# Attention probabilities transposed in 32x32 squares on VectorE and placed by SBUF-to-SBUF DMAs

## The chip, the cores and the metric

One Trainium2 chip; the kernel runs on one of its cores. The metric is the device time of one execution in microseconds (us), as the median over runs. The engines are TensorE (PE, its weight loads PEld), VectorE (DVE), ScalarE (ACT), GpSimd (POOL) and SyncE (SP, which issues the DMAs here).

## The reference

A trunk of two encoder layers on 512 tokens of 1024 features, in float32. In each layer one projection feeds three attention branches with heads of 64 features: A (4 heads, all 512 keys with a mask made of three dilated windows), B (8 query heads over 2 key heads, all keys, normalized and rotated queries and keys) and C (4 heads on an 8 x 64 grid, a window of 16 columns, learned bias). The branches are projected to 1024 features, gated, added up and projected again; a layer norm follows, then an MLP of 4096 hidden features and a second layer norm.

```
s = q @ k.T (+ mask or bias);  p = exp(s - max(s));  p = p / sum(p);  o = p @ v
merged = g0 * (oa @ w_branch_a) + g1 * (ob @ w_branch_b) + g2 * (oc @ w_branch_c)
x = layer_norm(alpha * x + merged @ w_out);  x = layer_norm(alpha * x + relu(x @ w_up)**2 @ w_down)
```

## The kernel before

Each float32 operand is split into a high part of TensorE's type F32R and the remainder (`Split`, hi and lo), and a product is three matmuls (`mm3`, lines 152 to 155). Weights come in chunks of 512 KB (`Stream`): SyncE loads a chunk into one of two raw buffers, ScalarE copies the high part (line 182), VectorE subtracts it (line 183). `advance`, called whenever a chunk is taken, splits one more chunk if a buffer is free; a chunk that is asked for and not ready is split on the spot. There are 5 split chunks in the pool `wts` and 3 in a second pool that exists outside attention only.

Attention in a layer goes through 64 slots in the order of a list: heads of A, then C, then B, and in each head four blocks of 128 queries. The order of instructions on every engine is that of the program. A slot does this, in order: the scores of the slot two ahead (`scores`: two matmuls, maximum on VectorE, exponential and sum on ScalarE); one chore; other matmul work (`work.pump(rate)`: projections, gates and branch products of A and C, in units of one `mm3`); the normalization of the tile two ahead (on GpSimd in A and B, on VectorE in C); in the first slot of a head the products with the values of the head before (`values`, 8 matmuls); the transposition of this slot's tile (`turn`); then again a chore and work. The rate is the number of units per call: 2.1 in A, 2.85 in C, 1.6 in B.

`turn` transposes each 128x128 block of the probabilities on TensorE into a PSUM bank (line 544; 4 blocks in A and B, 2 or 3 in C); ScalarE copies it out as `pth`, VectorE subtracts into `ptl`. Both tiles hold a whole head and have one buffer. `values` multiplies them with the values, and ScalarE and VectorE add up the two halves of the result into `of`. What is left of the work list runs after the last slot; then `tail` computes B's gates and products for each block of 128 features, with the last head's `values` after its fourth matmul step. GpSimd adds the gated branches up (line 617, `mg`). Then come the output projection and the MLP (`token_major` and the loop from line 838).

```
normalize = ahead(i + 2); chores.pump(); work.pump(rate[name]); normalize()
if qb == 0 and i: values(*slots[i - 1][:2])
turn(name, h, qb, probs.popleft())
chores.pump(); work.pump(rate[name])
```

Of the kernel before, what the change touches and what calls it, by code (L numbers as in the profile page):

```python
# [28 lines left out]
RAWS = 2  # L29
NEG = -1e30  # L30
# [98 lines left out]
def encoder(ctx: ExitStack, tc: tile.TileContext, x, x_t, w_qkv, w_c, w_gate, b_gate, qn, kn, rpb,  # L129
# [34 lines left out]
    class Stream:  # L164
# [10 lines left out]
        def split(self):  # L175
            raw, more, _ = self.issued.popleft()
            pool, n = (extra[0], 3) if more else (wts, 5)
            self.used[more] += 1
            hi = pool.tile([P, 1024], F32R, tag="whi", name="whi", bufs=n)
            lo = pool.tile([P, 1024], F32R, tag="wlo", name="wlo", bufs=n)  # L180
# [17 lines left out]
        def advance(self):  # L198
# [3 lines left out]
            while n and self.issued and self.issued[0][2] < self.turn:  # L202
                more = self.issued[0][1]
                if self.used[more] == (5, 3)[more]:
                    break
# [89 lines left out]
    def attention(l, keep, qk, open_heads):  # L295
# [16 lines left out]
        def project(n, evac, cost, before=None, order=None):  # L312
# [4 lines left out]
            for tb, i in order:  # L317
# [6 lines left out]
                for j in range(per):  # L324
                    k = i * per + j
                    mm3(ps[tb], xT[:, tb, k], w[i][:, j], k == 0, k == KB - 1)
                    yield cost
                if i == nw - 1:
                    if tb == TB - 1:
                        for c in w:  # L330
                            stream.free(c)
# [86 lines left out]
        def c_values(m):  # L418

            while m == 0 and "a" not in flags:  # L420
# [86 lines left out]
        def scores(name, h, qb):  # L507
# [9 lines left out]
            if name == "b":  # L517
                s = ps
                nc.vector.tensor_reduce(st[:, 0:1], ps, axis=AX.X, op=ALU.max)
            else:  # L520
                s = p
                add = maska[:, (3 - qb) * P:(3 - qb) * P + S] if name == "a" else bias[h][:, C_OFF[qb]:C_OFF[qb] + n]
                nc.vector.tensor_tensor_reduce(s, ps, add, 1.0, -3e38, ALU.add, ALU.max, st[:, 0:1])
            nc.vector.tensor_scalar(st[:, 1:2], st[:, 0:1], -1.0, None, op0=ALU.mult)
            nc.scalar.activation(p, s, AF.Exp, bias=st[:, 1:2], accum_out=st[:, 2:3])
# [23 lines left out]
        def values(name, h):  # L549
            v = {"a": lambda: V["a"][h // 2][:, :, h % 2], "b": lambda: V["b"][:, :, h // 4],  # L550
                 "c": lambda: V["c", h // 2][:, :, h % 2]}[name]()
            pt = pts["now"]
            po = bank("pso")
            order = (1, 2, 0, 3) if name == "c" else range(TB)
            for i, kb in enumerate(order):
                q0, q1 = keys_of(name, kb)
                sl = slice(q0 * P, q1 * P)
                nc.tensor.matmul(po[:, sl], v[:, kb], pt.hi[:, kb, sl], start=i == 0, stop=False, skip_group_check=True)
                nc.tensor.matmul(po[:, sl], v[:, kb], pt.lo[:, kb, sl], start=False, stop=i == TB - 1, skip_group_check=True)
# [4 lines left out]
            dst, a, b = of[half:half + HD], po[:HD], po[HD:]  # L564
            if name == "c":
                dst = by_columns(dst)
                a, b = blocks(a), blocks(b)
            nc.scalar.activation(dst, a, AF.Copy)
            nc.vector.tensor_tensor(dst, dst, b, op=ALU.add)
# [43 lines left out]
        def gated(name, m):  # L613
            t = keep.tile([P, S], F32, tag="t", name="t", bufs=2)
            yield from gate({"b": 1, "c": 2}[name], m, t)
            yield from branch(name, m, t)
            nc.gpsimd.tensor_tensor(merged[m], merged[m], t, op=ALU.add)

        def branch_c():
            for m in range(KB):  # L620
# [50 lines left out]
        rate = {"a": 2.1, "c": 2.85, "b": 1.6}  # L671
# [28 lines left out]
        for i, (name, h, qb) in enumerate(slots):  # L700
# [20 lines left out]
        stream.plan([a for m in range(KB) for a in g(1, [m]) + ([w_bb[l, m // 2]] if m % 2 == 0 else [])])  # L721

        def tail():
            steps = 0
            for m in range(KB):
                for _ in gated("b", m):
                    steps += 1
                    if steps == 4:
                        values(*slots[-1][:2])
# [36 lines left out]
    stream.plan([w_qkv[0, i] for i in range(6)])  # L766
# [15 lines left out]
    for l in range(L):  # L782
        with ExitStack() as left:
# [13 lines left out]
            stream.plan([w_out[l, k] for k in range(KB)], [0] * 4 + [1] * 3 + [0])  # L797
            for half in range(2):
                more = [int(m % 8 in (1, 4, 6)) for m in range(16)]
                stream.plan([w_up[l, half * 16 + m] for m in range(16)], more)  # L800
                stream.plan([w_down[l, half * 16 + m] for m in range(16)], more[:12] + [1] * 3 + [0])
            if l < L - 1:
                stream.plan([w_qkv[l + 1, i] for i in range(6)])
# [190 lines left out]
```

## Time and profile before

| | |
|---|---|
| Median of 3 runs | 1546.78 us (1545.64 to 1905.47) |
| Profiled execution | 1549.4 us, span 1547.6 us |
| TensorE busy | 1527.6 us, 7400 matmuls, mean granted clock 0.996 |
| VectorE, ScalarE, GpSimd busy | 866.0, 632.5, 182.0 us |
| DMA | 150.61 MB, mean 97 GB/s |

The span goes from the first to the last instruction, and the profiled execution's own time is 1.8 us more. Busy times of different engines overlap and do not add up; a busy TensorE may still hold pipelined matmuls with gaps too small to show. An idle engine costs nothing unless the one that ends the work waits for it. In layer 0 the slots of A run from about 53 to 121 us, those of C to 199, those of B to some 310; layer 1 repeats this from about 818.

### The profile page before, as it was taken

To read this page: it belongs to the slowest core of one execution; us is meant where nothing else is said; L and a number is where in the kernel's file an instruction comes from. 1 tells how busy PE (TensorE), PEld (TensorE's weight loads), DVE (VectorE), ACT (ScalarE), POOL (GpSimd) and SP (SyncE) were. 2 spreads that over 40 slices of the span, in tenths; PEclk is the share of its full clock that TensorE was granted. 3 is DMA by queue.
4 is the path that set the end of the run, shared out by engine and by line. 5 is a ranking of instruction groups with operands and counts; after the bars stand their busy time and mean duration, and the time that the engine had idled before them with its cause. 6 is when DMAs were issued, how large, how long until landed. Compare 5 with 4: busy or idle time off the path is not lost.

```text
span 1547.6 us, 19148 instructions
## 1 busy us (share of the span) xinstructions
PE 1527.6 (99%) x7400; PEld 1279.8 (83%) x7400; DVE 866.0 (56%) x1498; ACT 632.5 (41%) x1036; POOL 182.0 (12%) x190
## 2 busy tenths in 40 slices
PE   8999999999999999999999999999999999999997
PEld 6888888888898888888888888888888888888886
DVE  4678877644664314441566787776448542244315
ACT  4665666533144212431136556665332431134310
POOL 0113213211100000000102141233111000000001
PEclk9999999999999999999999999999999999999999
DMA  6222311153153323332331323112432432233311
GB/s 218 83 85 75 111 55 58 52 177 123 55 177 96 96 82 96 110 96 83 106 128 56 98 82 103 55 59 95 146 123 83 136 99 92 82 123 95 96 55 55
DMA packets 43434, 150.61 MB, mean 97 GB/s; under 512 B 5072, under 2 KB 5712, under 8 KB 43344
## 3 DMA queue, kind: packets, MB, share of 16 engines
q1 hardware_dynamic: 43344, 149.40, 30.5%
q8 instruction: 58, 0.95, 0.2%
q14 instruction: 32, 0.26, 0.1%
HBM read 145.19 MB, written 4.19 MB: 97 GB/s over the span
## 4 chain that ended last, share of the span: by engine, by line
PE 95%; DVE 2%; ACT 1%; DMA 1%; issue 0%; POOL 0%; SPq 0%; POOLq 0%; DVEq 0%; ACTq 0%
PE psd L155 9%; PE psd L154 9%; PE psd L153 9%; PE psu L154 8%; PE psu L155 8%; PE psu L153 8%; PE psg L155 6%; PE psg L154 6%; PE psg L153 6%; PE psp L544 3%; PE psq L155 2%; PE psq L153 2%; PE psq L154 2%; PE psb L155 2%; PE psb L153 2%; PE psb L154 2%
## 5 line engine op out<-in xcount | busy, mean ns | idle before, releaser
L183 DVE TENSOR_TENSOR wlo<-raw,whi 128x1024 fp32r<-128x1024 f32 (+1 forms) x246 | 306.9, 1248 | 421.5 <-ACT whi L182 420.5
L182 ACT ACTIVATE whi<-raw 128x1024 fp32r<-128x1024 f32 (+1 forms) x246 | 258.4, 1053 | 462.8 <-PE psd L155 143.1
L153 PE MATMUL psu<-xTh,whi 128*128 128x512 f32 (+1 forms) x576 | 210.8, 366 | 0.0
L154 PE MATMUL psu<-xTl,whi 128*128 128x512 f32 (+1 forms) x576 | 210.7, 366 | 0.0
L155 PE MATMUL psu<-xTh,wlo 128*128 128x512 f32 (+1 forms) x576 | 210.5, 365 | 0.0
L153 PE MATMUL psd<-whi,hh 128*128 128x512 f32 x512 | 199.3, 389 | 0.0
L155 PE MATMUL psd<-whi,hl 128*128 128x512 f32 x512 | 199.2, 389 | 0.0
L154 PE MATMUL psd<-wlo,hh 128*128 128x512 f32 x512 | 199.2, 389 | 0.0
L153 PE MATMUL psg<-xTh,whi 128*128 128x512 f32 x384 | 156.8, 408 | 0.0
L154 PE MATMUL psg<-xTl,whi 128*128 128x512 f32 x384 | 151.6, 395 | 0.0
L155 PE MATMUL psg<-xTh,wlo 128*128 128x512 f32 x384 | 151.6, 395 | 0.0
L154 PEld LDWEIGHTS psu<-xTl,whi 128*128 128x128 f32 x576 | 108.6, 189 | 17.7
L153 PEld LDWEIGHTS psu<-xTh,whi 128*128 128x128 f32 x576 | 108.6, 189 | 17.4
L155 PEld LDWEIGHTS psu<-xTh,wlo 128*128 128x128 f32 x576 | 108.6, 189 | 17.4
L266 POOL TENSOR_TENSOR ve<-ve,nhalf 128x1 f32<-128x1 f32 x16 | 24.2, 1513 | 775.0 <-DVE ve L265 775.0
L529 POOL TENSOR_SCALAR p<-p,stat 128x512 f32<-128x512 f32 x96 | 70.7, 737 | 360.2 <-DVE stat L528 242.9
L154 PEld LDWEIGHTS psd<-wlo,hh 128*128 128x128 f32 x512 | 96.1, 188 | 20.0
L153 PEld LDWEIGHTS psd<-whi,hh 128*128 128x128 f32 x512 | 96.1, 188 | 19.9
L155 PEld LDWEIGHTS psd<-whi,hl 128*128 128x128 f32 x512 | 96.1, 188 | 19.8
L153 PE MATMUL psq<-whi,xTh 128*128 128x512 f32 (+1 forms) x256 | 90.0, 351 | 7.2 <-ACT whi L182 6.7
L229 DVE TENSOR_TENSOR ptl<-psp,pth 128x512 fp32r<-128x512 f32 (+2 forms) x128 | 81.6, 637 | 21.2 <-ACT pth L228 19.8
L155 PE MATMUL psq<-whi,xTl 128*128 128x512 f32 (+1 forms) x256 | 87.9, 343 | 0.0
(116 smaller groups left out, 2572.7 us busy)
## 6 DMA issues: line engine op xcount, KB each, us to landing
raw<-in_w_up SPq DMA_DIRECT2D x64, 512.0 KB, 3.6
raw<-in_w_down SPq DMA_DIRECT2D x64, 512.0 KB, 3.5
raw<-in_w_gate SPq DMA_DIRECT2D x48, 512.0 KB, 3.5
raw<-in_w_qkv SPq DMA_DIRECT2D x22, 512.0 KB, 3.6
raw<-in_w_out SPq DMA_DIRECT2D x16, 512.0 KB, 3.6
raw<-in_w_c SPq DMA_DIRECT2D x12, 512.0 KB, 3.5
bias<-in_rpb SPq DMA_DIRECT2D x8, 640.0 KB, 3.9
raw<-in_w_bb SPq DMA_DIRECT2D x8, 512.0 KB, 3.6
```

The costliest lines, as they stand in the source:

```text
L153: nc.tensor.matmul(ps, lhs.hi, rhs.hi, start=start, stop=False)
L154: nc.tensor.matmul(ps, lhs.hi, rhs.lo, start=False, stop=False)
L155: nc.tensor.matmul(ps, lhs.lo, rhs.hi, start=False, stop=stop)
L182: nc.scalar.activation(hi[:, s], raw[:, s], AF.Copy)
L183: nc.vector.tensor_tensor(lo[:, s], raw[:, s], f32(hi[:, s]), op=ALU.subtract)
L229: nc.vector.tensor_tensor(dst.lo, ps, f32(dst.hi), op=ALU.subtract)
L266: nc.gpsimd.tensor_tensor(ve[:, 1:], ve[:, :1], nhalf[:, :1], op=ALU.pow)
L529: (nc.vector if name == "c" else nc.gpsimd).tensor_scalar(p, p, st[:, 3:4], 1.0, op0=ALU.mult, op1=ALU.mult)
L544: nc.tensor.transpose(ps[:, j * P:(j + 1) * P], p[:, j * P:(j + 1) * P], ident)
```

## The change

`turn` issues one VectorE transpose in squares of 32x32 from the probabilities into a tile `tx` (two of them, heads taking turns). After a head's fourth slot `gather` issues 16 DMAs of 64 KB (32 partitions, 4 pieces of 512 B each) on SyncE, which put the squares into their places in `ptl` (one buffer). In the second and third slot of the next head `settle` makes the high part from it: ScalarE copies into the `tx` tile just read, GpSimd subtracts in place. In the fourth slot `values` follows, just before the next `gather`; the last head's has two of B's gates ahead of it in `tail`, with DMAs on SyncE and ScalarE and half the subtractions on VectorE. For C GpSimd clears the squares outside the keys. The maximum is taken with its sign changed, which drops one VectorE instruction a slot, and C is normalized on GpSimd too. The weights have 4 + 4 split buffers in place of 5 + 3, and a chunk of a projection is freed as soon as its last use is issued. The rates are 2.75 in C and 1.5 in B.

```diff
-            pool, n = (extra[0], 3) if more else (wts, 5)
+            pool = extra[0] if more else wts
...
-                nc.vector.tensor_reduce(st[:, 0:1], ps, axis=AX.X, op=ALU.max)
+                nc.vector.tensor_reduce(st[:, 1:2], ps, axis=AX.X, op=ALU.max, negate=True)
...
-                (nc.vector if name == "c" else nc.gpsimd).tensor_scalar(p, p, st[:, 3:4], 1.0, op0=ALU.mult, op1=ALU.mult)
+                nc.gpsimd.tensor_scalar(p, p, st[:, 3:4], 1.0, op0=ALU.mult, op1=ALU.mult)
...
             if qb == 0:
-                pts["now"] = Split(pool.tile([P, TB, S], F32R, tag="pth", name="pth", bufs=1),
-                                   pool.tile([P, TB, S], F32R, tag="ptl", name="ptl", bufs=1))
-            pt = pts["now"]
+                pts["at"] = pts.get("at", 0) ^ 1
+                pts["sq"] = pool.tile([P, TB * 4, TB, SQ], F32, tag=f"tx{pts['at']}", name="tx", bufs=1)
...
+                            nc.gpsimd.memset(pts["sq"][:, 4 * kb:4 * kb + 4, a:b], 0.0)
             k0, k1 = keys_of(name, qb)
-            n = k1 - k0
-            ps = bank("psp")[:, :n * P]
-            for j in range(n):
-                nc.tensor.transpose(ps[:, j * P:(j + 1) * P], p[:, j * P:(j + 1) * P], ident)
-            split_psum(pt[:, k0:k1, qb * P:(qb + 1) * P], ps.rearrange("p (k q) -> p k q", q=P))
+            nc.vector.transpose(pts["sq"][:, 4 * k0:4 * k1, qb], p.rearrange("p (c a) -> p c a", a=SQ))
+
+        def gather(name, h, queues):
+            lo = pool.tile([P, TB, S], F32R, tag="ptl", name="ptl", bufs=1)
+            pts["lo"], pts["of"] = lo, pts["at"]
+            for n in range(16):
+                i, j = n % 4, n // 4
+                dst = f32(lo)[j * SQ:(j + 1) * SQ].rearrange("a k (i r) -> a k i r", i=4)[:, :, i]
+                src = pts["sq"][i * SQ:(i + 1) * SQ].rearrange("a (k j) q b -> a k j (q b)", j=4)[:, :, j]
+                queues[n % len(queues)].dma_start(dst, src)
...
+        def settle(name, kbs, engines=(nc.gpsimd, nc.gpsimd)):
+            if kbs[0] == 0:
+                pts["hi"] = pool.tile([P, TB, S], F32R, tag=f"tx{pts['of']}", name="pth", bufs=1)
+            for kb in kbs:
+                q = keys_of(name, kb)
+                hi, lo = (by_squares(pts[n][:, kb], *q) for n in ("hi", "lo"))
+                nc.scalar.activation(hi, f32(lo), AF.Copy)
+                engines[kb % 2].tensor_tensor(lo, f32(lo), f32(hi), op=ALU.subtract)
...
-            if qb == 0 and i:
-                values(*slots[i - 1][:2])
-                if (name, h) == ("a", 2):
-                    flags.add("a")
             turn(name, h, qb, probs.popleft())
+            if i >= TB:
+                before = slots[i - TB][:2]
+                if qb in (1, 2):
+                    settle(before[0], ((0, 1), (2, 3))[qb - 1])
+                if qb == TB - 1:
+                    values(*before)
+                    if before == ("a", 1):
+                        flags.add("a")
+            if qb == TB - 1:
+                gather(name, h, (nc.sync,) if i < len(slots) - 1 else (nc.sync, nc.scalar))
```

## Rows read from the trace of the kernel before

**Rows 1.** The page, part 1: busy time of each engine, share of the span.

```profile
PE 1527.6 (99%) x7400; PEld 1279.8 (83%) x7400; DVE 866.0 (56%) x1498; ACT 632.5 (41%) x1036; POOL 182.0 (12%) x190
```

**Rows 2.** The page, part 4: the chain of waits by line.

```profile
PE psd L155 9%; PE psd L154 9%; PE psd L153 9%; PE psu L154 8%; PE psu L155 8%; PE psu L153 8%; PE psg L155 6%; PE psg L154 6%; PE psg L153 6%; PE psp L544 3%; PE psq L155 2%; PE psq L153 2%; PE psq L154 2%; PE psb L155 2%; PE psb L153 2%; PE psb L154 2%
```

**Rows 3.** Busy time by stage, layer 0: heads A, C, B (window, us, engines, clock).

```profile
53.00:121.00 68.00, 67.92 (x374) 58.46 (x375) 48.87 (x120) 41.86 (x84) 10.44 (x16) 0.97 0.25 80
121.00:199.00 78.00, 78.00 (x388) 65.31 (x387) 63.36 (x151) 46.28 (x92) 22.81 (x22) 1.00 0.29 88
199.00:299.00 100.00, 100.00 (x501) 82.59 (x500) 74.50 (x152) 61.10 (x120) 28.45 (x34) 1.00 0.18 57
```

**Rows 4.** TensorE in order of time in B: start, us, engine, line, operation.

```profile
205.50 0.40 PE L155 MATMUL psb<-oh,wlo 128*128 128x512 f32 x1
205.73 0.60 PE L544 MATMUL psp<-ident,p 128*128 128x128 f32 x4
206.09 0.48 PE L153 MATMUL psb<-oh,whi 128*128 128x512 f32 x1
206.40 0.39 PE L154 MATMUL psb<-ol,whi 128*128 128x512 f32 x1
```

**Rows 5.** Waits of TensorE: who for whom, total us, times, longest.

```profile
PE psp L544 <- POOL p L529: 4.6, 2, 2.3
```

**Rows 6.** Busy time by 1 us after the first turn, with granted clock (PEclk).

```profile
54.00:55.00 1.00, 1.00 (x4) 0.81 (x3) 0.59 (x1) 0.37 (x1) 0.36 (x1) 0.50 0.91 348
...
56.00:57.00 1.00, 1.00 (x4) 0.81 (x3) 0.19 (x3) 0.74 (x2) 0.00 (x0) 0.50 0.00 0
```

**Rows 7.** Groups by line and shape: xcount, busy us, mean ns, idle before.

```profile
L183 DVE TENSOR_TENSOR wlo<-raw,whi 128x1024 fp32r<-128x1024 f32 x242 | 304.2, 1257 | 420.3 <-ACT whi L182 419.3
L182 ACT ACTIVATE whi<-raw 128x1024 fp32r<-128x1024 f32 x242 | 255.8, 1060 | 461.4 <-PE psd L155 143.1 <-DMA raw<-in_w_up 88.7 <-PE psu L154 87.6
...
L529 POOL TENSOR_SCALAR p<-p,stat 128x512 f32<-128x512 f32 x96 | 70.7, 737 | 360.2 <-DVE stat L528 242.9 <-DVE stat L524 90.9 <-PE pss L514 8.2
L229 DVE TENSOR_TENSOR ptl<-psp,pth 128x512 fp32r<-128x512 f32 x96 | 66.1, 689 | 20.4 <-ACT pth L228 19.5
...
L519 DVE TENSOR_REDUCE stat<-pss 128x1 f32<-128x512 f32 x64 | 43.8, 685 | 3.7 <-PE pss L514 3.3
...
L617 POOL TENSOR_TENSOR mg<-mg,t 128x512 f32<-128x512 f32 x32 | 43.8, 1369 | 158.6 <-DVE t L607 158.6
L228 ACT ACTIVATE hh<-r 128x512 fp32r<-128x512 f32 x64 | 40.4, 631 | 77.4 <-DVE r L844 77.4
```

**Rows 8.** Line 617 on GpSimd: duration ns minimum, median, maximum.

```profile
L617 POOL TENSOR_TENSOR mg<-mg,t x32: 1270/1290/2204, 234.7 to 1143.8; 128x512 f32<-128x512 f32 x32
```

**Rows 9.** GpSimd and VectorE in order of time after B's last head.

```profile
310.68 1.22 DVE L183 TENSOR_TENSOR wlo<-raw,whi 128x1024 fp32r<-128x1024 f32 x1
...
310.85 2.20 POOL L617 TENSOR_TENSOR mg<-mg,t 128x512 f32<-128x512 f32 x1 [4.23 <-DVE t L607]
```

**Rows 10.** SyncE's issues in order of time: start, us, tile, count.

```profile
783.53 0.40 SPq L655 DMA_DIRECT2D gqk<-in_qn  x1
...
784.97 0.38 SPq L501 DMA_DIRECT2D bias<-in_rpb  x1
```

**Rows 11.** DMA issues by tile: count, KB each, median us to landing.

```profile
x_dram<-x SPq DMA_DIRECT2D x8, 256.0 KB, 2.0
...
gqk<-in_qn SPq DMA_DIRECT2D x2, 64.0 KB, 3.9
```

**Rows 12.** First matmuls of `values`: a head's in A, C, B, B's last but one.

```profile
68.55 0.40 PE L558 MATMUL pso<-pth,v 128*128 128x512 f32 x1
...
120.91 0.40 PE L558 MATMUL pso<-pth,v 128*128 128x512 f32 x1
...
198.56 0.34 PE L558 MATMUL pso<-pth,v 128*128 128x384 f32 x1
...
299.27 0.39 PE L558 MATMUL pso<-pth,v 128*128 128x512 f32 x1
```

More of the change, by code (lines that the diff above doesn't have):

```diff
@@ L29 @@
 RAWS = 2
+AHEAD = 4
+FIRST = [1, 1, 0, 0, 0, 0]
+SQ = 32
 NEG = -1e30
@@ L203, in advance @@
                 more = self.issued[0][1]
-                if self.used[more] == (5, 3)[more]:
+                if self.used[more] == AHEAD:
                     break
@@ L418, in c_values @@
         def c_values(m):
-            while m == 0 and "a" not in flags:
+            while m == 0 and "a" not in flags or m == 1 and ("a", 1) not in oT:
                 yield None
@@ L556, in values @@
                 q0, q1 = keys_of(name, kb)
-                sl = slice(q0 * P, q1 * P)
-                nc.tensor.matmul(po[:, sl], v[:, kb], pt.hi[:, kb, sl], start=i == 0, stop=False, skip_group_check=True)
-                nc.tensor.matmul(po[:, sl], v[:, kb], pt.lo[:, kb, sl], start=False, stop=i == TB - 1, skip_group_check=True)
+                to = by_squares(po, q0, q1)
+                for n in ("hi", "lo"):
+                    nc.tensor.matmul(to, v[:, kb], by_squares(pts[n][:, kb], q0, q1), start=(i, n) == (0, "hi"),
+                                     stop=(i, n) == (TB - 1, "lo"), skip_group_check=True)
             half = (h % 2) * HD
@@ L565, in values @@
             if name == "c":
[L566 to L569, printed above, removed]
+                to = dst.rearrange("p (i r q c) -> p i r q c", i=4, r=2, q=TB)
+                cut = [(lambda t, r=r: t.rearrange("p (i q r c) -> p i r q c", i=4, q=TB, r=2)[:, :, r], to[:, :, r])
+                       for r in range(2)]
+            else:
+                cut = [(lambda t: by_squares(t, 0, TB), dst.rearrange("p (q i b) -> p i q b", q=TB, i=4))]
+            for f, to in cut:
+                nc.scalar.activation(to, f(a), AF.Copy)
+                nc.vector.tensor_tensor(to, to, f(b), op=ALU.add)
             if half:
@@ L619, in branch_c @@
         def branch_c():
+            while ("c", 1) not in oT:
+                yield None
             for m in range(KB):
@@ L720, in attention, with drain @@
         work.flush()
-        stream.plan([a for m in range(KB) for a in g(1, [m]) + ([w_bb[l, m // 2]] if m % 2 == 0 else [])])
-        def tail():
-            steps = 0
+        stream.plan(g(1, (0, 1)) + [w_bb[l, 0]])
+        stream.plan([a for m in range(2, KB) for a in g(1, [m]) + ([w_bb[l, m // 2]] if m % 2 else [])])
+        def drain(gen):
+            while True:
+                try:
+                    next(gen)
+                except StopIteration as e:
+                    return e.value
+        def tail():
+            last = slots[-1][:2]
+            settle(last[0], (0, 1), (nc.vector, nc.gpsimd))
+            ts = [drain(half_gate("b", 0))]
+            settle(last[0], (2, 3), (nc.vector, nc.gpsimd))
+            ts.append(drain(half_gate("b", 1)))
+            values(*last)
             for m in range(KB):
[L726 to L729, printed above, removed]
+                drain(gated("b", m, ts[m]))
+                if m + 2 < KB:
+                    ts.append(drain(half_gate("b", m + 2)))
                 yield merged[m]
@@ L765, in encoder @@
     xp = right.enter_context(tc.tile_pool(name="x", bufs=1, side="right", reuse_waits="tile"))
-    stream.plan([w_qkv[0, i] for i in range(6)])
+    extra[0] = right.enter_context(tc.tile_pool(name="early", bufs=1, side="right", reuse_waits="tile"))
+    stream.plan([w_qkv[0, i] for i in range(6)], FIRST)
     def split_x(tb, t, cut):
@@ L796, in encoder @@
             extra[0] = pool(right, "wts", "right")
-            stream.plan([w_out[l, k] for k in range(KB)], [0] * 4 + [1] * 3 + [0])
+            stream.plan([w_out[l, k] for k in range(KB)], [0, 1] * 4)
             for half in range(2):
-                more = [int(m % 8 in (1, 4, 6)) for m in range(16)]
-                stream.plan([w_up[l, half * 16 + m] for m in range(16)], more)
-                stream.plan([w_down[l, half * 16 + m] for m in range(16)], more[:12] + [1] * 3 + [0])
+                stream.plan([w_up[l, half * 16 + m] for m in range(16)], [0, 1] * 8)
+                stream.plan([w_down[l, half * 16 + m] for m in range(16)], [0, 1] * 8)
             if l < L - 1:
-                stream.plan([w_qkv[l + 1, i] for i in range(6)])
+                stream.plan([w_qkv[l + 1, i] for i in range(6)], FIRST)
             with ExitStack() as inner:
```

31 lines of the change are left out of this document (20 added, 11 removed).

## The prediction

> **What bounds the kernel now.** I read the busy times first: TensorE is busy for 99% of the span, and no other engine passes 56% [rows 1]. Busy can hide pipelining, so the chain of waits came next. Its sixteen costliest entries are all TensorE's, and the transposes of the probabilities (line 544) stand among them with 3% [rows 2]. The table by stage says the same of heads A, C and B: TensorE fills each stretch, and the fullest other engine is VectorE in C with 63.4 of 78 us [rows 3]. Whatever leaves TensorE comes off the end, until a new wait appears.
>
> **What is removed.** In the order of time, a group of four transposes takes 0.36 us before the next matmul starts, and that matmul runs 0.08 us longer than its neighbours' pitch of 0.23: 0.44 us a group, 0.11 a transpose [rows 4]. A layer has 64 in A, 40 in C (2 or 3 key blocks) and 128 in B: 232, with both layers 464, so 464 x 0.11 = **-51 us**; the chain's 3% of the span, 46, bears it out. The matmuls of `values` keep their number and columns.
>
> At the first turn of each layer TensorE waits for GpSimd's normalized tile, 4.6 us over both [rows 5], and then runs at the lower of its two levels, a granted clock of 0.50 (1.2 GHz) for some 3 us, losing about 1.5 us [rows 6]. Behind the transposes stood gate work that needs no probabilities, so this goes: 4.6 + 3 = **-7 us** (bounds 0 and -8).
>
> **What moves to other engines, at nothing while its cover holds.** VectorE loses the subtractions into `ptl` (0.69 us each) and gets one transpose per slot. The trace has no such transpose; the nearest rows are the one-input reduction of the same tile (0.69) and the 1024-column subtraction (1.26); I take 0.69, so its load hardly moves. ScalarE keeps four copies a head, at 0.63 from SBUF. GpSimd gets four subtractions a head at the `mg` addition's price, 1.29 us at the median and 1.37 on average, beside four normalizations at 0.74, and C's too [rows 7, 8]. TensorE's work in the slots is the cover for all of this; without it GpSimd's 5.2 us a head would be bare, which is what happens below.
>
> **Weights.** One split chunk fewer is ready during attention. `project` for the queries of B holds all four while it runs; the chunk after it is split only when it is asked for, which puts a copy of 1.06 and a subtraction of 1.26 [rows 7] in front of TensorE: up to 2.3 us in each layer, **+4 us** (bounds 0 and 5). Elsewhere two chunks stay ready, 16 units of three matmuls at 0.70 us, or 11 us. The 4 + 4 split in the MLP keeps as many chunks, and I cost it at nothing: the gaps it could open lie behind 4 ready chunks.
>
> **The new loop.** This decides. A head's 16 transfers write `ptl`, which has one buffer, so they wait until `values` of the head before has read it. `values` of this head then waits for the transfers, for ScalarE's copies and for GpSimd's subtractions. Nothing in that ring overlaps with itself, so successive heads cannot come closer than its length. SyncE waits there too: weight loads issued later stand behind its 16 transfers, up to 7.5 us, which the ready chunks cover. Its parts:
>
> - Transfers. Four issues that follow each other on SyncE start at 783.53 to 784.97, 0.48 us apart on average [rows 10]; I take 0.47. The last lands 2.0 us after its issue, as `x_dram<-x` does (SBUF as source, nothing ahead of it); `gqk`, 64 KB like these, needed 3.9 behind other loads [rows 11]. 15 x 0.47 + 2.0 = 9.05 us. Bounds: 7.7 (an issue's own 0.38, 2.0) and 11.0 (0.47, 3.9).
> - Settling. First copy 0.63 and a hand-over taken as 0.1, four subtractions at 1.29 in a row, one normalization of 0.74 that stands between the pairs in GpSimd's order: 6.6. Later gate additions and VectorE in the way: 0.4 more (bounds 0 and 1.4). 7.0.
> - The last matmul and its end, and SyncE's start: 0.23 + 0.39 = 0.6.
>
> Together **16.65 us** (C's last head has 10 of 16 blocks, so 2.0 less). Against it stands the time TensorE needs for a head. The first matmuls of `values` lie 17.45 us apart in A (three heads), 19.41 in C (four), 14.39 in B (seven) [rows 12]. Less the transposes (1.76, 1.10, 1.76) and, in C and B, four times 0.2 unit at 0.70 that the lower rate defers: 15.69, 17.75 and **12.07**. The deferred work runs later at the same cost. So C hides the loop, A nearly does, and B does not. In a layer, eight gaps between successive `values` fall into B's slots, one of them behind C's last head, and two into A's: 7 x (16.65 - 12.07) + (14.65 - 12.07) + 2 x (16.65 - 15.69) = 36.6 us, with both layers **+73 us**. A lower clock after such waits would cost about 1.5 us a head, inside the wait, so I add nothing.
>
> **Sum.** Against the profiled execution's 1549.4: -51 - 7 + 4 + 73 = 1568.4. That execution lies 2.6 us above the runs' median of 1546.78, so I predict **1566 us**, 1.2% slower: the gain is spent on waits in the B heads. With the lower bound of the transfers the loop is 15.3 and costs 46, or 1539.
>
> **Rivals.**
>
> *The loop is hidden.* If the transfers were issued much closer together or landed sooner, so that the ring fits into 12.1 us, only -51 - 7 + 4 remains: 1493 us, 3.5% faster. For it: TensorE now needs nothing from GpSimd to proceed within a head, and the slots have work. Against it: 5.2 us of subtractions and 0.6 of copy leave under 6 us for 16 issues that take 7 by [rows 10]. It needs overlap that I did not see; a part of it lies between 1493 and 1516 with a loop below 14.
>
> *The loop is longer, and the kernel slower.* Transfers of 128 pieces of 512 B land like `gqk`, 3.9 us after issue: the loop is 18.55. Then B loses 45.4 + 4.5, A 5.7 and C 4 x 0.8 = 3.2 a layer, 118 in all: 1610 us. The verdict turns at a loop of 17.2 us, where the sum passes 1578; that is 0.6 above my value. For it: GpSimd's additional work meets VectorE, and weight loads share the DMA engines. Against it: `gqk` queued behind larger loads.
>
> *GpSimd is blocked by VectorE.* The `mg` addition that started 0.17 us into a weight subtraction took 2.20 us, where 1.29 is usual [rows 9]: 0.9 lost. With about one and a half weight subtractions in a head's time, at worst 1.4 us join the loop, of which I have counted 0.4: +1.0 x 10 gaps x 2 = 20 us more, 1586. The Trainium skill (SBUF — State Buffer, Who interferes with whom) gives a rule by which a VectorE instruction with two SBUF inputs and a GpSimd instruction that reads SBUF exclude each other for a whole instruction. By that rule each subtraction that meets one waits it out; the 2.20 us agrees, the mean of 1.37 over 32 says that it is not the usual case.
>
> **Chances.** About 2% (31 us) is what a measurement of this kernel can tell from no change. My forecast, a loop of 14 to 17.2 us, 0.45; the longer loop 0.27 and blocking 0.10, both slower; the hidden loop 0.18. So faster 0.18, within 2% 0.45, slower 0.37. The range takes in the hidden loop (1493) and goes up to 1600; above it lies the far end of the longer loop, 1 to 1.5 in 10. The forecast's own range is 1520 to 1578.
>
> **What would show it.** No line 544; VectorE transposes of near 0.69 us. In B, `values` about 16.6 us apart instead of 12.1, TensorE idle some 4 us before the matmuls with `ptl`, put down to GpSimd's subtraction; ScalarE idle before the first settling copy, released by the transfer. SyncE issuing 16 transfers at 0.47. A and C without such gaps. I would be wrong if `values` in B come every 12 us, if the transfers take under 6 us, or if TensorE waits mainly for weights or for VectorE's transposes.

## The result and the profile after

The changed kernel takes 1675.82 us (median of 4 runs, 1675.29 to 1677.56) against 1546.21 of the kernel before on the same chip: a ratio of 1.0842, 95% interval 1.082 to 1.0863. It is 8.4% slower where 1.2% was forecast, outside the range. The span of the profiled execution is 1675.7 us, 128.1 more than before.

The page, part 1 (busy time of each engine):

```profile
PE 1556.6 (93%) x6936; PEld 1257.2 (75%) x6936; DVE 854.5 (51%) x1350; ACT 634.7 (38%) x1044; POOL 356.3 (21%) x378
```

TensorE executes 464 instructions fewer than in [rows 1], yet is busy for 29 us more, and its share falls from 99% to 93%. Idle TensorE time, span less busy, rises from 20.0 to 119.1 us. Busy time should have fallen by the 51 us of the transposes, to 1476.6; it is 80.0 above that. Most of it is the clock: a mean of 0.955 over 1675.7 us against 0.996 over 1547.6 is a loss of 75.4 against 6.2 us, 69 more (an estimate, as if that mean held for all of TensorE's work). So **99 us of new waits and 80 us of slower work** stand against the 51 saved.

The chain of waits by line:

```profile
PE psd L158 8%; PE psd L157 8%; PE psd L156 8%; PE psu L157 7%; PE psu L158 7%; PE psu L156 7%; POOL ptl L575 6%; SPq L561 6%; PE pso L588 4%; PE psg L156 2%; PE psg L157 2%; PE psg L158 2%; DVE wlo L186 2%; DMA raw<-in_w_gate 2%; PE psq L156 1%
```

Line 544 is gone from [rows 2]; the subtractions of the settling (line 575) and the transfers (561) have come in with 6% each. The table by stage in layer 0 (A, C, B, cut some 4 us behind each stage's last products; window, us, engines, clock), and below it three stretches inside one head of B:

```profile
53.00:150.00 97.00, 85.42 (x392) 67.38 (x391) 63.42 (x141) 52.16 (x105) 44.29 (x50) 0.93 0.39 114
150.00:233.00 83.00, 69.33 (x303) 55.56 (x302) 52.35 (x105) 42.43 (x88) 37.13 (x54) 0.92 0.43 116
233.00:392.00 159.00, 131.47 (x449) 92.88 (x449) 78.74 (x125) 66.62 (x124) 70.14 (x64) 0.85 0.39 107
...
283.40:285.70 2.30, 0.01 (x1) 0.01 (x1) 1.23 (x1) 2.11 (x4) 0.65 (x1) 1.00 0.69 143
285.70:291.60 5.90, 4.53 (x9) 2.24 (x10) 0.77 (x2) 1.50 (x3) 4.96 (x4) 0.70 0.40 142
291.60:294.00 2.40, 2.40 (x7) 1.82 (x7) 2.25 (x4) 0.83 (x2) 0.00 (x0) 0.50 0.15 34
```

Against [rows 3] TensorE no longer fills any stage: 85.4 of 97, 69.3 of 83, 131.5 of 159 us, and the clock falls to 0.85 in B. The last three rows show how: 2.3 us without work, 5.9 us of products that wait, and the stretch after them runs at 0.50, 1.2 GHz. TensorE's waits (total us, times, longest):

```profile
PE pso L588 <- ACT pth L574: 52.5, 24, 3.0
PE pso L588 <- POOL ptl L575: 42.4, 45, 5.4
```

The wait of [rows 5] is gone, and 94.9 us stand before the products instead, half for ScalarE's copies and half for GpSimd's subtractions. The new instructions by shape (busy us, mean ns), answering to [rows 7, 8], and then the transfers' landing, answering to [rows 11]:

```profile
L575 POOL TENSOR_TENSOR ptl<-ptl,pth 128x512 fp32r<-128x512 f32 x92 | 121.7, 1353 | 40.3 <-ACT pth L574 40.0 <-DMA raw<-in_w_qkv 0.2
...
L532 POOL TENSOR_SCALAR p<-p,stat 128x512 f32<-128x512 f32 x96 | 76.4, 797 | 278.0 <-DVE stat L531 278.0
...
L551 DVE STREAM_TRANSPOSE tx<-p 128x512 f32<-128x512 f32 x96 | 65.8, 701 | 81.6 <-PE pso L588 60.2 <-POOL p L532 16.2 <-POOL ptl L575 5.2
...
L574 ACT ACTIVATE pth<-ptl 128x512 fp32r<-128x512 f32 x96 | 52.6, 618 | 2.9 <-DMA ptl<-tx 2.7 <-issue 0.2
```

```profile
ptl<-tx SPq DMA_DIRECT2D x496, 64.0 KB, 2.0
```

All of these durations came out within some 0.06 us of the forecast. The first matmuls of `values`, for the same four heads as in [rows 12]:

```profile
74.16 0.39 PE L588 MATMUL pso<-pth,v 128*128 128x512 f32 x1
...
138.04 0.50 PE L588 MATMUL pso<-pth,v 128*128 128x512 f32 x1 [1.98 <-ACT pth L574]
...
225.15 0.44 PE L588 MATMUL pso<-pth,v 128*128 128x384 f32 x1 [2.42 <-ACT pth L574]
...
366.43 0.65 PE L588 MATMUL pso<-pth,v 128*128 128x512 f32 x1 [2.02 <-ACT pth L574]
```

They lie 21.3 us apart in A, 21.8 in C and 20.2 in B, where TensorE needs 15.69, 17.75 and 12.07: 5.6, 4.0 and 8.1 over. Over three, four and seven heads that is 89.7 us in layer 0; taking layer 1 alike, 179. With the other terms of the prediction the sum is 1549.4 - 51 - 7 + 4 + 179 = 1674, some 3 us short of the profiled execution's 1677.6. One head of B in order of time, all engines:

```profile
273.05 10.25 SPq L561 DMA_DIRECT2D ptl<-tx  x16
...
282.99 0.39 PE L158 MATMUL psg<-xTh,wlo 128*128 128x512 f32 x1
...
283.19 1.06 ACT L185 ACTIVATE whi<-raw 128x1024 fp32r<-128x1024 f32 x1 [1.35 <-PE psg L157]
...
284.15 0.67 ACT L620 ACTIVATE t<-psg,hb 128x512 f32<-128x512 f32 x1
...
285.01 2.19 ACT L574 ACTIVATE pth<-ptl 128x512 fp32r<-128x512 f32 x4 [0.19 <-issue]
...
285.69 0.49 PE L588 MATMUL pso<-pth,v 128*128 128x512 f32 x1 [2.32 <-ACT pth L574]
...
285.73 4.96 POOL L575 TENSOR_TENSOR ptl<-ptl,pth 128x512 fp32r<-128x512 f32 x4 [1.68 <-ACT pth L574]
...
287.06 0.50 PE L588 MATMUL pso<-ptl,v 128*128 128x512 f32 x1 [0.87 <-POOL ptl L575]
```

The transfers are issued back to back for 10.25 us, 0.64 each. ScalarE's first copy starts at 285.01, behind the gate's `tanh` (line 620) and a weight half (185) that both waited for TensorE, but also just when the last transfer lands: issued at some 282.7, it has 2.0 us to go by the median. TensorE finished its other work at 283.4 and has nothing else in its queue before the products: it waits 2.32 us for the first copy and then goes at the pace of four subtractions until 291.5. By microseconds, its clock falls to 0.50 at 288 and comes back at 295, so some 3.5 us of the next head's work run at the lower level too. Whether TensorE's work or the transfers hold the copies differs from head to head. These are a head of A and the copies of the next head of B:

```profile
79.32 10.63 SPq L561 DMA_DIRECT2D ptl<-tx  x16
...
95.71 2.19 ACT L574 ACTIVATE pth<-ptl 128x512 fp32r<-128x512 f32 x4
...
304.15 2.19 ACT L574 ACTIVATE pth<-ptl 128x512 fp32r<-128x512 f32 x4 [0.77 <-DMA ptl<-tx]
```

In A the copies start 5.8 us after the last issue has ended, without a wait for a transfer. In B ScalarE does wait for one in three heads running, 0.77, 0.21 and 0.68 us. There the loop ends last, at 18.7 to 19.4 us a head; in B's two longest gaps, of 25.1 and 23.5 us, the copies come 6 us behind the issues, straight after a `tanh`.

The program puts the copies in pairs in the second and third slot, with an exponential between the pairs. On ScalarE the four stand in one block behind them. The description of the kernel says that the order on every engine is the program's; for these copies that does not hold. The built order, below, is the one that each engine executes.

### The profile page after: what moved, and what is told of

It reads as the page before. It is cut to its first block, busy times and chain, and to the rows that moved or that the text cites. A ratio compares the mean times of both kernels' runs of the same rounds, so it can differ in the third digit from the quotient of the medians.

```text
span 1675.7 us, 19279 instructions
## 1 busy us (share of the span) xinstructions
PE 1556.6 (93%) x6936; PEld 1257.2 (75%) x6936; DVE 854.5 (51%) x1350; ACT 634.7 (38%) x1044; POOL 356.3 (21%) x378
## 4 chain that ended last, share of the span: by engine, by line
PE 66%; POOL 8%; DVE 7%; SPq 6%; DMA 5%; issue 4%; ACT 2%; ACTq 1%; POOLq 0%; DVEq 0%
PE psd L158 8%; PE psd L157 8%; PE psd L156 8%; PE psu L157 7%; PE psu L158 7%; PE psu L156 7%; POOL ptl L575 6%; SPq L561 6%; PE pso L588 4%; PE psg L156 2%; PE psg L157 2%; PE psg L158 2%; DVE wlo L186 2%; DMA raw<-in_w_gate 2%; PE psq L156 1%
## 5 line engine op out<-in xcount | busy, mean ns | idle before, releaser
L532 POOL TENSOR_SCALAR p<-p,stat 128x512 f32<-128x512 f32 (+2 forms) x128 | 95.5, 747 | 350.3 <-DVE stat L531 341.7
L575 POOL TENSOR_TENSOR ptl<-ptl,pth 128x512 fp32r<-128x512 f32 (+2 forms) x124 | 149.6, 1237 | 43.0 <-ACT pth L574 42.8
L156 PE MATMUL psg<-xTh,whi 128*128 128x512 f32 x384 | 153.2, 399 | 0.0
L551 DVE STREAM_TRANSPOSE tx<-p 128x512 f32<-128x512 f32 (+2 forms) x128 | 81.5, 651 | 103.3 <-PE pso L588 70.5
L588 PE MATMUL pso<-ptl,v 128*128 128x512 f32 (+2 forms) x128 | 76.6, 601 | 49.2 <-POOL ptl L575 42.4
L588 PE MATMUL pso<-pth,v 128*128 128x512 f32 (+2 forms) x128 | 62.8, 492 | 52.5 <-ACT pth L574 52.5
L157 PEld LDWEIGHTS psd<-wlo,hh 128*128 128x128 f32 x512 | 96.1, 188 | 19.9
L156 PEld LDWEIGHTS psd<-whi,hh 128*128 128x128 f32 x512 | 96.1, 188 | 19.9
```

Source lines behind the costliest of these rows:

```text
L156: nc.tensor.matmul(ps, lhs.hi, rhs.hi, start=start, stop=False)
L157: nc.tensor.matmul(ps, lhs.hi, rhs.lo, start=False, stop=False)
L532: nc.gpsimd.tensor_scalar(p, p, st[:, 3:4], 1.0, op0=ALU.mult, op1=ALU.mult)
L551: nc.vector.transpose(pts["sq"][:, 4 * k0:4 * k1, qb], p.rearrange("p (c a) -> p c a", a=SQ))
L575: engines[kb % 2].tensor_tensor(lo, f32(lo), f32(hi), op=ALU.subtract)
L588: nc.tensor.matmul(to, v[:, kb], by_squares(pts[n][:, kb], q0, q1), start=(i, n) == (0, "hi"), stop=(i, n) == (TB - 1, "lo"), skip_group_c ...
```

## The experiments

My theory after the trace: a head's settling stands at the very end of the slots' work in ScalarE's order, so that TensorE's slot work and the settling add up instead of overlapping, and the clock that falls in each wait stretches the sum (**sum**). The rival: it is the loop of transfers and settling alone, longer than I had it (**ring**). In B the two should come out nearly alike, 12.07 + 6.5 for the sum and 18.7 for the loop; A and C, 21.3 and 21.8 us a head, lie above the loop. A second rival: the other parts of the change (weights, maxima). Here is what each run did to waits and slow work; idle time is over the 20.0 us of before, slow work is TensorE's busy time over 1476.6 (for the first row over 1527.6), both from the profiled execution.

| Kernel | Median us | Ratio to before (95%) | Idle | Slow work |
|---|---|---|---|---|
| weights and scores alone (e1) | 1551.96 | 1.0017 to 1.004 | 3 | 0 |
| **changed kernel** | 1675.82 | 1.082 to 1.0863 | 99 | 80 |
| 8 transfers (e2) | 1672.77 | 1.0795 to 1.0831 | 95 | 80 |
| subtractions on two engines (e3) | 1627.33 | 1.0506 to 1.0538 | 84 | 43 |
| two `ptl` (e4) | 1667.23 | 1.0754 to 1.0802 | 98 | 75 |
| copies held in place (e5) | 1679.63 | 1.0831 to 1.0863 | 103 | 77 |
| the same, 8 transfers (e6) | 1657.65 | 1.0683 to 1.0719 | 88 | 74 |
| rows of 2 KB (e7) | 1674.44 | 1.0795 to 1.0827 | 94 | 78 |
| e3 + e5 + e7 (e8) | 1630.81 | 1.0519 to 1.055 | 85 | 48 |
| one transfer (e9) | 1567.6 | 1.0108 to 1.0138 | 42 | 27 |
| no settling (e10) | 1557.26 | 1.0048 to 1.0082 | 44 | 15 |
| products a head later, two `ptl` (e11) | 1631.05 | 1.0503 to 1.0567 | 75 | 62 |
| two queues (e16) | 1648.22 | 1.063 to 1.0676 | 92 | 63 |
| e11 + e16 + e3 (e14) | 1584.99 | 1.0218 to 1.027 | 59 | 28 |
| e14, copies held in slot 3 (e13) | 1608.69 | 1.0369 to 1.0407 | 77 | 35 |
| e11 + e3, held in slot 4 (e15) | 1571.14 | 1.0126 to 1.0162 | 48 | 22 |
| e15, two queues (e19) | 1583.49 | 1.0218 to 1.0254 | 60 | 23 |
| e15, weights from ScalarE (e17) | 1563.3 | 1.0084 to 1.0114 | 49 | 16 |
| e15, weights from GpSimd (e18) | 1587.7 | 1.024 to 1.0273 | 68 | 22 |

**The other parts alone (e1).** The kernel before with 4 + 4 weight buffers, early freeing, the sign-changed maximum and C's normalization on GpSimd; transposes stay on TensorE.

> The kernel before, with its TensorE transposes and its order of slots, plus the other edits of the change: 4 + 4 split buffers with alternating pools, chunks freed one by one, the negated maximum, C normalized on GpSimd. Ring theory (the period of a head is set by transfers, settling and values through the one ptl buffer): the loss is all in that ring, so this stays within 1540 to 1556 us. Weights theory (TensorE and ScalarE starve because one chunk fewer is ready): at least 1570 us, with TensorE waiting for whi or wlo in attention.

1551.96 against 1547.7 us: +4. The weights are not the cause, and the forecast's +4 for them has the right size: this trace has a new wait of 4.3 us for weight halves, while the wait of [rows 5] falls to 0.5.

**Half the issues (e2).**

```diff
-            for n in range(16):
+            for n in range(8):     # 128 KB each
```

> The changed kernel with 8 transfers of 128 KB a head in place of 16 of 64 KB: the same bytes, half the issues; the squares land in wrong places, so the result is not the attention. Ring theory: the transfers take 7 x 0.64 + 2.1 = 6.6 us in place of 12.0, heads of B come some 13 to 14 us apart in place of 18.5 to 20, A and C gain 2 to 4 us a head: 1530 to 1590 us. If the DMA engines' work and not the issue sets the transfers: above 1650. If the order in which ScalarE and GpSimd come to the settling sets it: above 1620.

Only 3 us less. The same stretch of B in this run:

```profile
271.71 5.40 SPq L561 DMA_DIRECT2D ptl<-tx  x8
...
281.19 1.06 ACT L185 ACTIVATE whi<-raw 128x1024 fp32r<-128x1024 f32 x1 [1.39 <-PE psg L157]
...
282.15 0.67 ACT L620 ACTIVATE t<-psg,hb 128x512 f32<-128x512 f32 x1
...
282.73 2.18 ACT L574 ACTIVATE pth<-ptl 128x512 fp32r<-128x512 f32 x4
...
283.39 0.50 PE L588 MATMUL pso<-pth,v 128*128 128x512 f32 x1 [2.01 <-ACT pth L574]
```

The issue takes 5.40 us instead of 10.25, and still the copies start 5.6 us after it, again behind the weight half and the `tanh` that wait for TensorE. From the first head of B to the last, the products lie 19.9 us apart on average (20.2 before), though the loop is now some 14 us (eight issues, 2.6 of landing, the settling) and TensorE's own time 12.07, or 14.6 with 2.5 us of slow work. So the period is not the larger of the two, and the ring by itself is not the limit.

**Subtractions on two engines (e3), two placed tiles (e4).**

```diff
-        def settle(name, kbs, engines=(nc.gpsimd, nc.gpsimd)):
+        def settle(name, kbs, engines=(nc.vector, nc.gpsimd)):       # e3
-            lo = pool.tile([P, TB, S], F32R, tag="ptl", name="ptl", bufs=1)
+            lo = pool.tile([P, TB, S], F32R, tag="ptl", name="ptl", bufs=2)    # e4; 3 + 4 weight buffers
```

> The changed kernel with half of the settling subtractions of every head on VectorE (as it does for the last head only). Ring theory: four GpSimd subtractions in a row (5.0 us) become two beside two of VectorE (2.7 us), so each of about 14 gaps a layer that the ring sets shortens by 2 us: 1610 to 1630 us. If the wait is for ScalarE's copies or the transfers alone: above 1660.

> The changed kernel with two ptl buffers; paid for by 3 in place of 4 split chunks in the attention pool, and B's query projection goes chunk by chunk, so that it needs one at a time. Ring theory: transfers no longer wait for values of the head before, the ring is open, heads of B come 12.1 to 13.5 us apart (the issue of 16 transfers, 10.3 us, then is the nearest bound), A and C at 15.7 and 17.8: 1495 to 1540 us. If the placing of settling in the engines' queues or the weights set the time: 1600 or more.

e3 gives 48 us, 1.5 a gap: the settling is on TensorE's path. Of the 52 us between the two profiled executions, 15 are idle time and 37 slow work. e4 opens the ring and gives 8.

**Copies held at their place (e5, e6, e8).** Whatever ScalarE and GpSimd get later in the program is issued behind the copies and subtractions of the third slot.

```diff
+            for c in held.values():
+                stack.enter_context(tc.issue_after(c))
...
+            with behind():
+                normalize = ahead(i + 2)
...
```

> The changed kernel, with one thing forced: a head's four copies and four subtractions stand in the third slot of the next head, and whatever of ScalarE and GpSimd comes later in the program is issued behind them. Sum theory (the settling stands last in ScalarE's queue, so TensorE's slot work and the settling add up): A and C come back to about their TensorE time (A 17 to 18 us a head, C 18), while B is still held by the ring of 18.5 us that the transfers' 10.25 us of issue make, so about 110 to 125 us of gaps remain of 187: 1605 to 1630 us. Ring theory (the order costs nothing, only transfers and settling count): no change, 1660 to 1680 us. If the forced order itself blocks ScalarE (exponentials wait behind copies that wait for landings): above 1680 us.

> The run with 8 transfers of 128 KB a head instead of 16 of 64 KB (squares placed so that the output is not the attention), with the forced order of the settling added. Sum theory: both limits are gone, the ring is 5.1 + 2.0 + 6.5 = 13.6 us, so B stands at 13.6 to 15 us a head, A and C at their TensorE time: 1510 to 1560 us. If neither the order nor the ring is the limit (a third cause, such as the lower clock by itself or GpSimd's occupancy): as without the forced order, 1650 to 1675 us.

> The changed kernel with the squares and the placed tile laid out so that each of the 16 transfers is 32 rows of 2 KB on both sides, the same 64 KB, order of settling untouched. The issue of one should fall from 0.60 us to 0.35 to 0.45 us, so 16 take 6 to 8 us instead of 10.25. Sum theory: the time hardly moves, as with 8 transfers: 1650 to 1676 us. Ring theory: each of the 32 gaps shrinks by 2 to 4 us: 1550 to 1610 us. If the issue time is a matter of the SBUF-to-SBUF path and not of the number of pieces, the issue stays at 0.60 us and both give 1676.

> Rows of 2 KB, forced order, and the settling's subtractions alternating between VectorE and GpSimd. Sum theory: ring about 7 + 2 + 4.3 = 13.3 us, B at 13.5 to 15 us a head, A and C at their TensorE time; 1495 us plus 1.5 to 3 us in 16 heads of B and up to 10 us elsewhere: 1500 to 1550 us, which would be faster than the kernel before or level with it. If a third cause holds the heads apart: 1600 us and more.

e5 and e6 missed, and with them the sum theory as I had put it, by the copies' place alone; e8 gives no more than e3 does. The hold touches ScalarE's and GpSimd's order, not TensorE's: in e6 the copies of one head start at 315.07 behind a `tanh` of 314.48, 6 us after the last issue, and TensorE, done at 314.5 with all the work that stands before the products, waits again. Holding the copies is no cure while the products follow them directly. e7 moved the time by 1 us, but it can't tell the theories apart: the issue stays at 0.63 us with a quarter of the pieces, so the loop is no shorter (the start and the duration of 16 issues):

```profile
270.91 10.01 SPq L562 DMA_DIRECT2D ptl<-tx  x16
```

**One transfer (e9), no settling (e10).**

```diff
+            queues[0].dma_start(dst, src)                # e9: one of 1 MB for 16
-                nc.scalar.activation(hi, f32(lo), AF.Copy)                                      # e10
-                engines[kb % 2].tensor_tensor(lo, f32(lo), f32(hi), op=ALU.subtract)
```

> The changed kernel with one transfer of 1 MB a head, squares copied straight to the placed tile, instead of 16 of 64 KB; so the squares stand in the wrong places and the output is not the attention. Settling and its order are untouched. One issue of some 0.4 us takes the place of 10.25 us, and the ring is about 0.4 + 4 + 6.5 = 11 us, under TensorE's time of every head. Ring theory: all gaps close, 1495 to 1530 us. Sum theory (TensorE does a head's slot work, then waits through the settling, whatever the transfers take): near the run with 8 transfers, 1640 to 1672 us.

> The changed kernel with the four copies and four subtractions a head left out: the values products read the placed tile, unsplit, for both halves, so the output is not the attention to the reference's precision. The 16 transfers stay. Sum theory: only the transfers are left between heads, 10.25 + 2 + 0.6 = 12.9 us against 12.07 in B, so B stands at 13 to 14.5 us a head and A and C at their TensorE time: 1500 to 1545 us. Ring theory: the same ring of 12.9 us and so the same time; with the run of one transfer beside it the two are told apart. If neither (the clock, the weights' order or VectorE's transposes hold the heads apart): 1600 us and more.

e10 lies 12 us above the range that both theories gave, so it does not tell them apart; but 119 us of the 130 go with eight instructions a head. What is left in B is the transfers' own ring, with the product's wait for a landing:

```profile
245.05 2.08 PE L587 MATMUL pso<-ptl,v 128*128 128x512 f32 x8 [1.22 <-ACT t L619]
...
259.63 2.96 PE L587 MATMUL pso<-ptl,v 128*128 128x512 f32 x8 [3.72 <-DMA ptl<-tx]
```

The two heads are 14.6 us apart; between them lie 10.54 of issue, 2.0 of landing and 2.1 of products. e9 is 108 us faster than the change, which the sum theory as I had put it excluded (1640 to 1672); it is also 38 us above the range of the loop alone. Its trace:

```profile
265.32 0.47 SPq L559 DMA_DIRECT2D ptl<-tx  x1
...
271.12 0.67 ACT L618 ACTIVATE t<-psg,hb 128x512 f32<-128x512 f32 x1
...
271.69 0.63 ACT L572 ACTIVATE pth<-ptl 128x512 fp32r<-128x512 f32 x1
...
272.96 0.69 ACT L528 ACTIVATE p<-pss,stat 128x512 f32<-128x512 f32 x1
...
273.64 1.66 ACT L572 ACTIVATE pth<-ptl 128x512 fp32r<-128x512 f32 x3
...
277.05 0.39 PE L586 MATMUL pso<-pth,v 128*128 128x512 f32 x1
...
280.39 0.50 PE L586 MATMUL pso<-ptl,v 128*128 128x512 f32 x1 [1.47 <-POOL ptl L573]
```

The copies no longer stand in one block at the end: one is at 271.69, three at 273.64, and exponentials lie between them. The products start 5 us after the first copy with TensorE's work in between, and 1.47 us of waiting are left. So the built order itself changed with the number of transfers. e9 changes two things, the transfers' real time and the place of the copies; e2, which changes the first alone, says that the first is worth little while the second stays.

**Products a head later (e11), two queues (e16), and both (e14, e13, e15).** In e11 `values` stands in the second slot of the head after next, with that head's first two transposes behind it.

```diff
+            if i >= 2 * TB and qb == 1:
+                values(*slots[i - 2 * TB][:2])
+            while qb >= 1 and turns:
+                turn(*turns.popleft())
...
-                gather(name, h, (nc.sync,) if i < len(slots) - 1 else (nc.sync, nc.scalar))
+                gather(name, h, (nc.sync, nc.scalar))        # e16, e14, e13, e19
```

> The changed kernel with two placed tiles (weight ring of 3 chunks ahead instead of 4 in one pool) and the values products another step later: in the second slot of the head after next, with that head's first two transposes behind them. Nothing is left out. The settling of a head then has the whole of the next head's TensorE work beside it and some slots more. Sum theory: TensorE waits for no settling, B at 12 to 14 us a head: 1495 to 1540 us, faster than the kernel before or level with it. Ring theory: two placed tiles and the later products open the ring too, so it gives the same, though two tiles by themselves gave only 8 us. If the order puts the settling late again or the weight ring starves: 1580 us and more.

In e11 the copies moved back along with the products:

```profile
276.53 10.25 SPq L562 DMA_DIRECT2D ptl<-tx  x16
...
302.48 2.19 ACT L575 ACTIVATE pth<-ptl 128x512 fp32r<-128x512 f32 x4
```

The last transfer is issued at 286.8, the copies come 15.7 us later. They stand just ahead of the products wherever these are, and 1631 us is far above the 1540 expected.

> The changed kernel with every head's 16 transfers issued from SyncE and ScalarE in turn, 8 each; nothing else. Theory of the place in the queue (the order laid down takes the transfers to land late and puts the copies last before the products): two queues let the order expect them earlier, copies move up between the exponentials, TensorE's slot work covers a part of the settling: 1585 to 1640 us. If only the ring's real length counted: with 8 transfers the issue was halved too and gave 3 us, so 1665 to 1680 us, a little more by ScalarE's 5 us of issue a head.

> Two placed tiles, the values products in the second slot of the head after next, two issuing queues, subtractions on VectorE and GpSimd in turn. Nothing is left out. Place theory: transfers land about 7 us into a head, the copies stand half a head ahead of the products, TensorE waits for little: B at 12 to 14 us a head, 1510 to 1565 us. If waits for ScalarE (its issues block exponentials and weight halves) take their place: 1600 us and more.

> The same, with all four copies and subtractions put in the third slot of the next head and what comes later on their engines held behind them. Place theory: as the run without the force or up to 20 us better, 1495 to 1560 us. If the force makes ScalarE wait for transfers that have not landed, exponentials and weight halves come late: above that run by 20 us and more.

> Two placed tiles, products in the second slot of the head after next, the settling forced into the last slot of the next head, all 16 transfers on SyncE. The transfers land 12.25 us into the next head, which in B is its whole TensorE time of 12.07, so ScalarE waits for landings at the forced place: B at 13 to 16 us, 1530 to 1600 us by the place theory, above the run with two queues by 20 to 50 us. If the speed of the transfers does not count, level with the run with two queues.

Two queues alone give 28 us, between what the two theories expected. The copies are spread out, but ScalarE's own issues now stop it, as its rows show:

```profile
266.06 1.46 ACTq L561 DMA_DIRECT2D ptl<-tx  x2
...
268.85 4.40 ACTq L561 DMA_DIRECT2D ptl<-tx  x6
...
273.63 0.69 ACT L528 ACTIVATE p<-pss,stat 128x512 f32<-128x512 f32 x1 [4.16 <-DMA ptl<-tx]
```

Eight issues take it 5.9 us, and the exponential starts only 0.4 us after the last of them. The 4.16 us of idle time before it, put down to a transfer, are nearly all the issues' own time. With the products later as well, e14 comes to 1585, 20 us above what was expected. Best of these is e15, with one queue, two engines for the subtractions and the copies held in the last slot: the order of the two was the reverse of what I expected, and e13 is 37 us slower. It differs in two things, the slot and the second queue; e19, which differs from e15 in the queue alone, puts 12 of the 37 down to that. TensorE's waits in e15:

```profile
PE psg L158 <- DVE wlo L186: 18.5, 9, 4.9
PE psg L156 <- ACT whi L185: 17.6, 6, 3.7
PE pso L597 <- POOL ptl L582: 4.8, 6, 1.6
PE pso L597 <- ACT pth L581: 3.2, 4, 1.3
```

The settling is down from 94.9 to 8.7 us, the waits for VectorE's subtractions included. In its place stand weight halves, 36.1 us. SyncE in the same run:

```profile
245.72 11.19 SPq L568 DMA_DIRECT2D ptl<-tx  x16
257.01 0.53 SPq L197 DMA_DIRECT2D raw<-in_w_gate  x1
257.65 10.45 SPq L568 DMA_DIRECT2D ptl<-tx  x16
```

**What is left (e17, e18, e19).** The transfers fill SyncE: the next 16 start 11.9 us after these, with one weight chunk in between.

```diff
-                    nc.sync.dma_start(raw[:, s], src[:, s])
+                    nc.scalar.dma_start(raw[:, s], src[:, s])      # e17; nc.gpsimd in e18
```

> The run with two tiles, products in the head after next, forced settling and one queue for the transfers, with the weight chunks' loads issued by ScalarE instead of SyncE. If SyncE's full queue makes the weights late: the 36 us of waits for weight halves shrink to 10 or less, 1530 to 1555 us. If the weight ring of 3 is what makes them late: unchanged, 1560 to 1575. If ScalarE's own waits delay the loads: 1580 us and more.

> The same with the weight loads issued by GpSimd. If SyncE's queue makes the weights late: 1530 to 1560 us, less what issuing costs GpSimd, which no run shows. If the ring of 3: 1560 to 1575. If GpSimd's issues cost it more than a microsecond each or wait behind its subtractions: 1580 us and more.

> The same run with each head's transfers on SyncE and ScalarE, 8 each, weight loads on SyncE. If SyncE's queue makes the weights late: 1535 to 1560 us. If ScalarE's 5 us of issues a head block its exponentials and weight halves: 1575 to 1610 us, as the run with the settling forced a slot earlier (1609).

e17 gains 8 us, less than expected; the other two lose 12 and 17. TensorE's waits for weight halves fall from 36.1 to 27.2 us in e17, where 10 or less were expected. So a full SyncE explains a part only. Its time lies in the range given for the weight ring of three chunks, a rival that no run changes by itself. Three gaps of B in layer 0 are 12.0, 12.2 and 12.8 us in e17, near the forecast's TensorE time: there the settling and the transfers are hidden. The four others are 13.8 to 21.5. The best version with the transposes on VectorE and the whole computation, 1563.3 us, is still 1.0% slower than the kernel before.

Open stays why the built order puts the copies just before the products when there are 16 or 8 transfers on one queue and earlier with one transfer or with two queues (an estimate of the transfers' time in the making of the order would do it; none of these runs sees it), how much of e15's gain over e11 is the hold and how much the second engine, and what the waits for weights in e17 come from.

## Why the prediction was wrong

- *Transposes, -51.* Borne out: in e10, where few waits are left, TensorE's busy time is 14.8 us above 1476.6, and the mean clock (0.988 over 1555.5 us, less the 6.2 of before) explains 12.5 of it.
- *First turn, -7, and weights, +4.* Right as far as seen: the wait is gone, what the clock behind it gave back no run separates, and e1 measures +4 for all of the other parts together.
- *Durations.* Transposes 0.70 (0.69 said), copies 0.62 (0.63), subtractions 1.35 on average (1.29 to 1.37), normalizations 0.80 (0.74), landing 2.0 (2.0). Only the issue was mis-sized, 0.64 instead of 0.47: the ring was 10.25 + 2.0 + 6.5, about 18.7 us, in place of 16.65. The second rival's 18.55 is near it by luck: it came from a landing of 3.9 us, and 2.0 was measured.
- *The step that failed* is the period of a head as the larger of TensorE's time and the loop, in two sentences. "C hides the loop, A nearly does, and B does not": they are 4.0, 5.6 and 8.1 us over. What was to hide the settling, TensorE's work in the slots, stands ahead of it in the queues, so TensorE's time and the settling add up. In B the mis-sized loop is as long as that sum and ends last in some heads; in A and C the sum is the longer. e3 (-48) and e10 (-119) show that the settling lies bare, e2 and e4 (-3, -8) that a shorter or an open ring alone does not cover it. I had read the order of instructions from the program. The trace of before could not show the copies' place, and I gave it no rival.
- "A lower clock after such waits would cost about 1.5 us a head, inside the wait, so I add nothing": the slow work is 80 us, 2.5 in each of 32 heads, 69 of it by the estimate above the clock. It would lie inside the wait if the loop ran independently of TensorE. Here the copies wait for the `tanh` of work that TensorE does at the lower clock, so slower work makes the next settling later. That is the larger miss: 99 us of idle time stand against 73 forecast, 80 of slow work against nothing. The second rival's 118 us are near the 99, in part by luck again, since it gave A and C 8.9 us a layer where 32.9 were lost; its 1610 lacks the clock.
- *Slips in the sums* that decide nothing: 4.6 + 3 is 7.6; the loop of 15.3 costs 48 us, not 46; a loop of 14 us gives 1520, not 1516; and the second rival charges C with 18.55 us, though C's loop had been put 2.0 lower.
- *GpSimd blocked by VectorE* was small. The subtractions' mean of 1353 ns against the 1290 of [rows 8] is 0.3 us a head. Where both engines subtract at once, behind the last head, VectorE's and GpSimd's pairs lasted 3.47 and 3.17 us:

```profile
382.81 3.17 POOL L575 TENSOR_TENSOR ptl<-ptl,pth 128x512 fp32r<-128x512 f32 x2 [7.32 <-ACT pth L574]
...
383.06 3.47 DVE L575 TENSOR_TENSOR ptl<-ptl,pth 128x512 fp32r<-128x512 f32 x2
```

VectorE's subtraction of this size is 0.69 alone [rows 7]. The Trainium skill (SBUF — State Buffer, Who interferes with whom) has such a pair exclude each other for whole instructions. GpSimd starts 0.25 us earlier, so by that rule VectorE's pair would take an estimated 1.04 + 0.69 + 1.29 + 0.69 = 3.71 us; with 3.47 measured, this trace agrees to a quarter of a microsecond.

## What to carry to other kernels

A cover counts only if it stands behind the covered work in the built order of every engine that both use: find in a trace which instruction stands just ahead of the new one, and if the order can't be seen, price the sum of the two beside the larger one. When waits like these (2.32, 0.87 and 0.49 us in the head shown) recur in each step on TensorE, price the lower clock behind them as a term of its own: here the slow work is 0.8 of the added idle time, in the other runs with VectorE's transposes 0.3 to 0.8. Where two limits are about equal, lift both in one run before either is ruled out.

## What the runs showed of the hardware

- A transfer from SBUF to SBUF takes its queue 0.63 to 0.68 us on average, with 128 pieces of 512 B or 32 rows of 2 KB, and at 64 or 128 KB; one of 1 MB over 128 partitions took 0.47. A weight chunk of 512 KB takes 0.33 at the least on SyncE, 0.53 beside transfers in the rows above, 0.33 to 0.36 on ScalarE (e17), and 0.53 to 0.72 on GpSimd, as in this row of e18:

```profile
248.48 0.60 POOL L197 DMA_DIRECT2D raw<-in_w_bc  x1
```

- In the head of B shown above, the clock stayed at 0.50 for some 7 us behind waits of 2.32, 0.87 and 0.49 us.
- Where VectorE and GpSimd subtracted two tiles of 128x512 each at the same time, VectorE's two took 3.47 us, in place of 0.69 each.
